# Sums of squares for keys and queries: squares of transposed blocks on ScalarE in place of products with a column of ones

## The chip, the cores and the metric

The kernel runs on one core of one Trainium2 chip. The metric is the device time of one execution in microseconds, here the median of three runs. TensorE does the matrix products (PE in the profile, its weight loads PEld), VectorE is DVE, ScalarE is ACT, GpSimd is POOL, and SP issues the DMAs. All engines run in order; the kernel fixes the order on each of them when it is built.

## What is computed

One decoder layer on x of 1024 tokens by 1024 channels, fp32: a gated DeltaNet branch with 8 heads and a sparse attention branch with 8 heads, merged by gates, an output product, and an MLP of width 4096. The change lies in the DeltaNet branch, in the L2 norm of its queries and keys over the 128 channels of a head:

```python
def l2_normalize(x):
    xf = x.astype(jnp.float32)
    return xf * lax.rsqrt(jnp.sum(xf * xf, axis=-1, keepdims=True) + EPS)
...
    qkv = jax.nn.silu(causal_short_conv(g_qkv, conv_w))
    gq, gk, gv = jnp.split(qkv, [GDN_QK_DIM, 2 * GDN_QK_DIM], axis=-1)
    gq = l2_normalize(gq.reshape(B, S, GDN_HEADS, GDN_HEAD_K)) * (GDN_HEAD_K ** -0.5)
    gk = l2_normalize(gk.reshape(B, S, GDN_HEADS, GDN_HEAD_K))
...
    o_gdn = gated_delta_rule_chunked(gq, gk, gv, g, beta)
```

## The kernel before, in words

The input projection is made in units of 128 or 256 columns, each a chain of products in PSUM tiles called `dd`. For the DeltaNet branch there are 48 units (per head: key `k`, query `q`, value `v`, and the gates `z`, `a`, `b`). Every fp32 operand is split into a high and a low part, so one K-tile of 128 takes three products of 512 columns, and a half unit takes 24 (`gdense`, line 711).

A key, query or value unit goes through `conv` (line 760): ScalarE copies the two halves out of PSUM into `cu`, ScalarE and VectorE make the causal convolution of four taps, ScalarE the Tanh and VectorE the product that is SiLU. The result (`kt`, `qt` or `t` in the profile) has channels on partitions and the 1024 tokens along the free axis. For keys and queries `conv` then takes the sums of squares over the channels, that is over partitions (lines 800 to 812): ScalarE squares the whole tile into `cu` (128x1024), TensorE multiplies each of the eight blocks of 128 tokens with a column of ones (`one`, 128x1) into a tile of the PSUM ring `tt`, and VectorE reads the eight columns of sums, adds epsilon (4 * EPS) and gives the tile back. Then `conv` is done, and `keys` (line 823), `queries` (line 982) or `values` (line 1002) of that head starts.

`keys` fetches a row of decays by DMA (`es`), has ScalarE make the decay matrix, takes the reciprocal root of the sums (`rsq_w`), the products of keys with keys (`tt<-kt`), and hands 32x32 blocks through DRAM to a solve on POOL (`sx`, `stmp`, `um`). `join` puts the blocks of the inverse together (`jj`). `decayed` transposes the keys (`tt<-ident,kt`) for the state's update. `queries` makes the products of queries with keys (`tt<-qt,kt`). `scan` (line 1024) is the recurrence over 8 chunks of a head: `cc` and `oo` on TensorE, `sr` and `sst` on VectorE, `svn`, `sqs` and a square with an accumulator (`gj`) on ScalarE. `output` (line 1078) uses the queries' sums once more, transposes and writes the head out.

The ring `tt` (class `Ring`, two PSUM tiles) is shared by all of these. A chain waits for a free tile (`yield tt.ready`), takes it (`tt.get`) and frees it behind the last reader.

The order of all engines is made by a planner (`Weave`, line 2011). Each step above is a Python generator; the planner keeps a time of its own, books a duration for each instruction by a fixed formula, and takes the ready chain with the smallest priority number. `gdense` has the last priority, 9: its `dd` products fill the time in which no other chain has work for TensorE. What an instruction does on the chip in longer time than the formula makes the plan late there, as the engines follow the planned order and not the planned times. The formulas that matter here:

```python
                if op == "matmul" and not fast and "tile_position" not in kw:
                    return wv.issue(name, ins, (n * 1.67 + 5) / 1e3, 0.25)
...
                return wv.issue(name, ins, (n * (0.417 if fast else 0.835) + (13.4 if wv.shared else 2.5)) / 1e3, 0.25)
...
                return wv.issue(name, ins, 0.13 + n / 1200 + (0.1 if "accum_out" in kw else 0), 0.15)
```

The first is an fp32 product of n columns on TensorE (for n = 1 it books 0.007 us), the second an F32R product or a transpose, the third a ScalarE activation of n elements per partition.

Of the kernel before, what the change touches and what calls it, by code (L numbers as in the profile page):

```python
# [9 lines left out]
F32 = mybir.dt.float32  # L10
F32R = mybir.dt.float32r
BF16 = mybir.dt.bfloat16
F16 = mybir.dt.float16
I32 = mybir.dt.int32
AF = mybir.ActivationFunctionType
OP = mybir.AluOpType
# [4 lines left out]
P = 128  # L21
S = 1024
D = 1024
NB = S // P
# [4 lines left out]
EPS = 1e-6  # L29
# [21 lines left out]
def body(tc, a, out, dbg=None):  # L51
    nc = tc.nc
    ctx = ExitStack()
    V, A, G, PE, SY = nc.vector, nc.scalar, nc.gpsimd, nc.tensor, nc.sync
# [23 lines left out]


    padl, padl_es = pool("padl", side="left")  # L80
    G.memset(padl.tile([P, 24], F32, name="padl"), 0.0)
    cst, cst_es = pool("cst", side="left")
    dr, dr_es = pool("dr", space=DRAM)
    htp, ht_es = pool("htp", side="left")
# [14 lines left out]
    V_, A_, G_, PE_, SY_ = (wv.engine(e, n) for e, n in ((V, "V"), (A, "A"), (G, "G"), (PE, "PE"), (SY, "SY")))  # L99

    def rsq_w(pl, dst, src, n, tag):
        t = pl.tile([P, n], F32, name=tag + "t")
        V_.tensor_scalar(dst.bitcast(I32), src.bitcast(I32), -0.5, float(0x5F3759DF), op0=OP.mult, op1=OP.add)
        for _ in range(3):
            yield
            V_.scalar_tensor_tensor(t, dst, -0.5, src, op0=OP.mult, op1=OP.mult)
            yield
            V_.tensor_tensor(t, t, dst, op=OP.mult)
            yield
            V_.scalar_tensor_tensor(dst, t, 1.5, dst, op0=OP.add, op1=OP.mult)  # L110
# [10 lines left out]
    ident = cst.tile([P, P], F32, name="ident")  # L121
    vecs = cst.tile([P, NV], F32, name="vecs")
    g025 = cst.tile([P, 1], F32, name="g025")
    one = cst.tile([P, 1], F32, name="one")
    dtb = cst.tile([P, H], F32, name="dtb")
    alg = cst.tile([P, H], F32, name="alg")
    nss, nms, nr = (cst.tile([P, NB], F32, name=n) for n in ("nss", "nms", "nr"))
# [31 lines left out]
    def loads():  # L159
        SY_.dma_start(ident, a["c_ident"])  # L160
        after(("ident",))
        for half in range(2):
            if half == 0:
                ts = [ix.tile([P, NB, 256], F32, name="pj", bufs=2).rearrange("p a b -> p (a b)") for _ in range(2)]
                xs.extend(t[:, o:o + D] for t in ts for o in (0, D))
            else:
                xs.extend([slot(1, [P, D], F32), slot(5, [P, D], F32)]
                          + [ix.tile([P, D], F32, name="irl", bufs=2) for _ in range(2)])
            for tb in range(4 * half, 4 * half + 4):
                SY_.dma_start(xs[tb], x[tb * P:(tb + 1) * P, :])  # L170
                after(("x", tb))
            if half == 0:
                SY_.dma_start(vrow[0:96], a["conv_w"][0].rearrange("j (t p) -> (j t) p", p=P))
                SY_.dma_start(vrow[96:104], a["norm_mix_g"][0].rearrange("(t p) -> t p", p=P))
                SY_.dma_start(vrow[104:112], a["norm_mlp_g"][0].rearrange("(t p) -> t p", p=P))
                SY_.dma_start(vrow[112:113], a["gdn_norm_g"])
                after(("vrow",))
                load(0)
                after(("raw", 0))
        load(1)  # L180
        after(("raw", 1))
        SY_.dma_start(ropeI, a["c_ropei"])
        SY_.dma_start(dtb, a["dt_bias"].to_broadcast([P, H]))
        SY_.dma_start(alg, a["a_log"].to_broadcast([P, H]))
        SY_.dma_start(triu, a["c_triu"])
        G_.memset(ones, 1.0)
        G_.memset(one, 1.0)
        SY_.dma_start(ropeA, a["c_ropea"])
        SY_.dma_start(qng, a["q_norm_g"].to_broadcast([P, P]))
        SY_.dma_start(kng, a["k_norm_g"].to_broadcast([P, P]))  # L190
        yield


    def after(key):
        wv.add(0, later(wv.busy["SY"] + SY_LATENCY, key))
# [471 lines left out]
    blk = lambda t, b: t[:, b * P:(b + 1) * P]  # L667
# [92 lines left out]
    def conv(u):  # L760
        h, c = gunits[u]
        ct = ctile[c] + h
        yield ("gp",)
        if len(convs) > 1:
            yield ("conv", convs[-2])
        convs.append(u)
        cu = gq.tile([P, 3 + S], F32, name="cu", bufs=2)
        G_.memset(cu[:, 0:3], 0.0)
        for half in range(2):
            yield ("half", (u, half))  # L770
            wv.add(-1, cdrain(cu, u, half))
            yield ("drained", u, half)
        cw = [vecs[:, j * 24 + ct:j * 24 + ct + 1] for j in range(4)]
        if c == "k" and h > 2:
            yield ("out", h - 3)
        if c == "k" and h > 1:
            yield ("keys", h - 2)
        if c == "q" and h > 1:
            yield ("scan", h - 2)
        if c == "q" and h > 2:  # L780
            yield ("out", h - 3)
        if c == "v" and h:
            yield ("values", h - 1)
        yield
        o = (gq if c == "v" else gp).tile([P, S], F32, name={"k": "kt", "q": "qt", "v": "t4"}[c],
                                          bufs={"k": 3, "q": 2, "v": 1}[c])
        A_.activation(o, cu[:, 0:S], AF.Copy, scale=cw[0])
        for j in range(1, 4):
            yield
            yield "V"  # L790
            V_.scalar_tensor_tensor(o, cu[:, j:j + S], cw[j], o, op0=OP.mult, op1=OP.add)
        yield
        yield "A"
        A_.activation(cu[:, 0:S], o, AF.Tanh, scale=0.5)
        yield
        yield "V"
        V_.scalar_tensor_tensor(o, cu[:, 0:S], 1.0, o, op0=OP.add, op1=OP.mult)
        yield
        st[h][c + "t"] = o
        if c != "v":  # L800
            yield "A"
            A_.activation(cu[:, 0:S], o, AF.Square)
            yield
            yield tt.ready
            ps, slot_ = tt.get()
            for b in range(NB):
                PE_.matmul(ps[:, 0, b:b + 1], blk(cu, b), one, start=True, stop=True)
            yield
            st[h][c + "ss"] = gp.tile([P, NB], F32, name=c + "ss", bufs=3)
            V_.tensor_scalar(st[h][c + "ss"], ps[:, 0, 0:NB], 4 * EPS, None, op0=OP.add)  # L810
            tt.free(slot_)
            yield
        wv.done("conv", u)
        wv.add(2, {"k": keys, "q": queries, "v": values}[c](h))

# [7 lines left out]
    def keys(h):  # L823
# [9 lines left out]
        SY_.dma_start(es.rearrange("p b c -> p (b c)"), GC[h:h + 1, :].to_broadcast([P, S]))  # L833
        dma = ("es", h)
        after(dma)
        yield dma
        for b in range(NB):
            A_.activation(es[:, b, :], es[:, b, :], AF.Abs, bias=ngc[:, b, h:h + 1])
# [2 lines left out]
            if b % 4 == 3:  # L841
                A_.activation(es[:, b - 3:b + 1, :], es[:, b - 3:b + 1, :], AF.Exp, scale=-1.0)
        rk = gp.tile([P, NB], F32, name="rk", bufs=2)
        yield from rsq_w(gp, rk, st[h]["kss"], NB, "rk")
        ck = gp.tile([P, NB], F32, name="ck", bufs=2)
        av = gp.tile([P, NB], F32, name="av", bufs=3)
        nb_ = gp.tile([P, NB], F32, name="nb", bufs=3)
# [55 lines left out]
            SY_.dma_start(um[32 * q:32 * q + 32, :, 32 * q:32 * q + 32], zu[q])  # L903
        yield
        wv.add(1, join(h))


    def decayed(h):
# [73 lines left out]
    def queries(h):  # L982
        qt = st[h]["qt"]
        yield ("keys", h)
        if h > 1:
            yield ("out", h - 2)
        kt, aq = st[h]["kt"], st[h]["aq"]
        for half in range(2):
            hs = slice(half * 4, half * 4 + 4)
            yield tt.ready  # L990
            ps, slot_ = tt.get()
            for i in range(4):
                b = half * 4 + i
                PE_.matmul(ps[:, i, :], blk(kt, b), blk(qt, b), start=True, stop=True)
            yield
            V_.tensor_tensor(aq[:, hs, :], ps, aq[:, hs, :], op=OP.mult)
            tt.free(slot_)
            yield
        wv.done("queries", h)
# [78 lines left out]
    def output(h):  # L1078
        yield ("gate", (h, "a"))
        oss, qss, oo, og = (st[h][k] for k in ("oss", "qss", "vv", "kt"))  # L1080
        fo = gp.tile([P, NB], F32, name="fo", bufs=2)
        fe = gp.tile([P, NB], F32, name="fe", bufs=2)
        V_.tensor_scalar(fe, qss, 128 * EPS, None, op0=OP.mult)
        yield
        V_.scalar_tensor_tensor(fe, oss, 1.0 / P, fe, op0=OP.mult, op1=OP.add)
        yield
        yield from rsq_w(gp, fo, fe, NB, "fo")
        yield
        V_.tensor_tensor(oo, oo, fo[:, :, None].to_broadcast([P, NB, P]), op=OP.mult)
        yield  # L1090
        for half in range(2):
            yield tt.ready
            ps, slot_ = tt.get()
            for i in range(4):
                PE_.transpose(ps[:, i, :], oo[:, half * 4 + i, :], ident)
            yield
            hs = slice(half * HALF, (half + 1) * HALF)
            V_.scalar_tensor_tensor(og[:, hs], ps.rearrange("p a b -> p (a b)"), g025, zzs[h][:, hs],
                                    op0=OP.mult, op1=OP.mult)
            tt.free(slot_)  # L1100
            yield
        SY_.dma_start(M1[h // 4][h % 4], og)
        yield
        wv.done("out", h)
# [1088 lines left out]
```

## Time and profile before

| | |
|---|---|
| median of 3 runs | 1859.11 us (1858.0 to 1859.21) |
| profiled execution, its own time | 1857.71 us |
| its span | 1856.0 us |
| TensorE busy | 1827.3 us (98%) |
| VectorE busy | 1263.4 us (68%) |
| ScalarE busy | 1005.1 us (54%) |
| POOL busy | 548.8 us (30%) |

Read it so: the busy share is an average over the span. Matmuls are pipelined, and the profile models their ends, so two records of TensorE can overlap, and the distance from one start to the next is what a product really takes. The DeltaNet heads run from about 270 to 965 us, the attention and the MLP behind them. Nearly all instructions are issued through one helper and so carry one line number; they are told apart by the names of their tiles, as output<-moving operand, stationary operand for TensorE.

### The profile page before, as it was taken

How to read it: one execution, taken by the hardware profiler on the slowest of the kernel's cores; microseconds unless marked ns; L12 is line 12 of the kernel's file. 1: busy time of each engine (PE TensorE's matmuls, PEld its weight loads, DVE VectorE, ACT ScalarE, POOL GpSimd, SP SyncE). 2: the span in 40 equal slices, each digit the busy share in tenths (PEclk: the TensorE clock that was granted, in tenths of full speed). 3: DMA queues.
4: the chain of work that ended last, by engine and by line, in shares of the span. 5: the costliest groups of instructions: out<-in, count | busy, mean ns of one | idle time of the engine just before them, and what ended most of it. 6: DMA issues, size and time to landing. Idle time of an engine off the chain costs nothing.

```text
span 1856.0 us, 28461 instructions
## 1 busy us (share of the span) xinstructions
PE 1827.3 (98%) x10406; PEld 1560.9 (84%) x10406; DVE 1263.4 (68%) x2615; ACT 1005.1 (54%) x2022; POOL 548.8 (30%) x752
## 2 busy tenths in 40 slices
PE   8899999999999999999999999999999999999999
PEld 7889998888888888888888888877888888888887
DVE  4557757757677777865348767677866667957655
ACT  6556646646566555354237666666666665333330
POOL 0214640542524516356003311231232322222210
PEclk8999999999999999999999999999999999999999
DMA  4102232233122222321336412222644459453423
GB/s 160 47 25 68 69 103 57 63 90 78 50 69 58 58 57 69 87 63 49 86 122 212 147 60 66 80 97 75 208 143 155 157 180 328 150 188 102 125 79 137
DMA packets 190510, 195.65 MB, mean 105 GB/s; under 512 B 36593, under 2 KB 140322, under 8 KB 190370
## 3 DMA queue, kind: packets, MB, share of 16 engines
q1 hardware_dynamic: 190370, 193.83, 33.3%
q8 instruction: 82, 1.34, 0.3%
q14 instruction: 58, 0.48, 0.1%
HBM read 139.62 MB, written 54.17 MB: 104 GB/s over the span
## 4 chain that ended last, share of the span: by engine, by line
PE 93%; DVE 3%; ACT 1%; issue 1%; POOL 0%; DMA 0%; SPq 0%; DVEq 0%; POOLq 0%; ACTq 0%
PE dd L2122 54%; PE o L2122 14%; PE s L2122 7%; PE pt L2122 6%; PE tt L2122 4%; PE cc L2122 2%; PE jj L2122 2%; PE sq L2122 2%; PE oo L2122 1%; DVE w L2122 1%; DVE rqs L2122 1%; PE tp L2122 0%; DVE sc L2122 0%; DMA pj<-in_x_dram 0%; POOL hl L2122 0%
## 5 line engine op out<-in xcount | busy, mean ns | idle before, releaser
L2122 PE MATMUL dd<-hh,w 128*128 128x512 f32 x1568 | 521.3, 403 | 0.9 <-ACT hh L2122 0.9
L2122 PEld LDWEIGHTS dd<-hh,w 128*128 128x128 f32 x1568 | 288.8, 189 | 52.2 <-ACT hh L2122 1.3
L2122 PE MATMUL dd<-hl,w 128*128 128x512 f32 x784 | 316.2, 403 | 0.6 <-DVE hl L2122 0.6
L2122 PE MATMUL dd<-w,hh 128*128 128x256 f32 x960 | 182.8, 287 | 0.0
L2122 ACT ACTIVATE m<-m 128x512 f32<-128x512 f32 (+1 forms) x240 | 140.0, 625 | 76.6 <-PE dd L2122 32.4
L2122 PE MATMUL dd<-hh,m 128*128 128x512 f32 x520 | 172.0, 395 | 1.0 <-DVE w L2122 0.8
L2122 PEld LDWEIGHTS dd<-hl,w 128*128 128x128 f32 x784 | 148.1, 189 | 26.5 <-DVE hl L2122 1.5
L2122 DVE TENSOR_TENSOR m<-m,m 128x512 fp32r<-128x512 f32 (+2 forms) x177 | 134.9, 790 | 36.1 <-ACT m L2122 33.0
L2122 PEld LDWEIGHTS dd<-w,hh 128*128 128x128 f32 x960 | 154.8, 194 | 1.5
L2122 PE MATMUL dd<-w,hl 128*128 128x256 f32 x480 | 137.4, 286 | 0.0
L2122 POOL TENSOR_TENSOR sx<-sx,stmp 128x60 f32<-128x60 f32 (+24 forms) x248 | 114.4, 461 | 19.4
L2122 PEld LDWEIGHTS dd<-hh,m 128*128 128x128 f32 x520 | 96.7, 188 | 20.5 <-DVE w L2122 2.4
L2122 POOL TENSOR_TENSOR stmp<-sx,um 128x60 f32<-128x60 f32 (+24 forms) x186 | 82.9, 446 | 76.0 <-DMA um<-ZA 62.6
L2122 POOL TENSOR_TENSOR m<-m,m 128x512 f32<-128x512 f32 x48 | 67.6, 1417 | 126.3 <-ACT m L2122 62.1
L2122 DVE TENSOR_SCALAR_CACHE_REDUCE tkeq<-sc,cand 128x384 f16<-128x384 f32 (+3 forms) x128 | 103.3, 807 | 1.4
L2122 PE MATMUL dd<-hl,m 128*128 128x512 f32 x260 | 102.3, 393 | 0.9 <-POOL hl L2122 0.9
L2122 DVE TENSOR_TENSOR w<-w,w 128x1024 fp32r<-128x1024 f32 (+1 forms) x56 | 65.4, 1172 | 47.1 <-ACT w L2122 47.1
L2122 PEld LDWEIGHTS dd<-w,hl 128*128 128x128 f32 x480 | 93.2, 194 | 0.1
L2122 ACT ACTIVATE ha<-m 128x1024 fp32r<-128x1024 f32 x43 | 43.8, 1054 | 80.0 <-PE s L2122 35.3
L2122 ACT ACTIVATE hh<-m 128x1024 fp32r<-128x1024 f32 x40 | 40.7, 1055 | 75.1 <-PE o L2122 37.6
L2122 ACT ACTIVATE w<-w 128x1024 fp32r<-128x1024 f32 x48 | 50.8, 1058 | 55.1 <-PE dd L2122 52.2
L2122 PE MATMUL o<-hh,m 128*128 128x512 f32 x248 | 80.3, 391 | 0.0
(468 smaller groups left out, 4456.2 us busy)
## 6 DMA issues: line engine op xcount, KB each, us to landing
HD<-m SPq DMA_DIRECT2D x106, 256.0 KB, 2.3
m<-HD SPq DMA_DIRECT2D x53, 512.0 KB, 3.9
w<-in_w_in_dram SPq DMA_DIRECT2D x48, 512.0 KB, 4.0
m<-in_w_mlp_up_dram SPq DMA_DIRECT2D x33, 512.0 KB, 5.1
wraw<-in_w_in_dram SPq DMA_DIRECT2D x8, 1024.0 KB, 5.3
m<-in_w_mlp_down_dram SPq DMA_DIRECT2D x16, 512.0 KB, 4.4
w<-in_x_dram SPq DMA_DIRECT2D x10, 512.0 KB, 4.9
hh<-in_w_mlp_down_dram SPq DMA_DIRECT2D x10, 512.0 KB, 4.7
```

The costliest lines, as they stand in the source:

```text
L2122: ins = f(*args, **kw)
```

## The change

The sums are taken at another place and by other engines. `conv` ends with the SiLU. A new helper `squares` transposes the eight blocks of a key or query tile, four to a tile of the ring `tt`, so that tokens are on partitions; ScalarE squares each block of 128x128 from PSUM and adds up along the free axis with its accumulator (`accum_out`). `keys` calls it behind the issue of the decay row, `queries` at its start. Epsilon is added by an extra operation for the keys (`ke`) and inside an operation that was there for the queries (`fe`). The column of ones goes; the pad at the start of SBUF grows from 24 to 32 columns.

```diff
-    G.memset(padl.tile([P, 24], F32, name="padl"), 0.0)
+    G.memset(padl.tile([P, 32], F32, name="padl"), 0.0)
...
         st[h][c + "t"] = o
-        if c != "v":
-            yield "A"
-            A_.activation(cu[:, 0:S], o, AF.Square)
-            yield
-            yield tt.ready
-            ps, slot_ = tt.get()
-            for b in range(NB):
-                PE_.matmul(ps[:, 0, b:b + 1], blk(cu, b), one, start=True, stop=True)
-            yield
-            st[h][c + "ss"] = gp.tile([P, NB], F32, name=c + "ss", bufs=3)
-            V_.tensor_scalar(st[h][c + "ss"], ps[:, 0, 0:NB], 4 * EPS, None, op0=OP.add)
-            tt.free(slot_)
-            yield
         wv.done("conv", u)
...
         after(dma)
+        kss = gp.tile([P, NB], F32, name="kss", bufs=2)
+        yield from squares(kt, kss)
         yield dma
...
-        yield from rsq_w(gp, rk, st[h]["kss"], NB, "rk")
+        ke = gp.tile([P, NB], F32, name="ke", bufs=2)
+        V_.tensor_scalar(ke, kss, 4 * EPS, None, op0=OP.add)
+        yield
+        yield from rsq_w(gp, rk, ke, NB, "rk")
...
+    def squares(t, ss):
+        for half in range(2):
+            yield tt.ready
+            ps, slot_ = tt.get()
+            for i in range(4):
+                PE_.transpose(ps[:, i, :], blk(t, half * 4 + i), ident)
+            yield
+            for i in range(4):
+                b = half * 4 + i
+                junk = gp.tile([P, P], BF16, name="gj")
+                A_.activation(junk, ps[:, i, :], AF.Square, accum_out=ss[:, b:b + 1])
+                if i % 2:
+                    yield
+            tt.free(slot_)
...
         kt, aq = st[h]["kt"], st[h]["aq"]
+        qss = st[h]["qss"] = gp.tile([P, NB], F32, name="qss", bufs=3)
+        yield from squares(qt, qss)
...
-        V_.tensor_scalar(fe, qss, 128 * EPS, None, op0=OP.mult)
+        V_.tensor_scalar(fe, qss, 4 * EPS, 128 * EPS, op0=OP.add, op1=OP.mult)
```

Since the planner books other durations and other chains, the order moves on every engine between the first key and the end of the last head's recurrence. On TensorE the first 1803 rows and the last 3588 rows of the order (rows of equal instructions merged) are the same before and after. The first place is TensorE at the first key's sums, among the `dd` products of the next unit; before:

```order
L2122 MATMUL dd<-hl_113,w_3182 128x512
L2122 MATMUL dd<-hh_112,w_3183 128x512
L2122 MATMUL tt<-one,cu 128x1 x8
L2122 MATMUL dd<-hh_98,w_3182 128x512
L2122 MATMUL dd<-hl_99,w_3182 128x512
L2122 MATMUL dd<-hh_98,w_3183 128x512
L2122 MATMUL dd<-hh_100,w_3182 128x512
L2122 MATMUL dd<-hl_101,w_3182 128x512
L2122 MATMUL dd<-hh_100,w_3183 128x512
L2122 MATMUL dd<-hh_102,w_3182 128x512
L2122 MATMUL tt<-ident,kt 128x128 x4
```

With the change, the second half of the same key (the first half stands 15 `dd` products earlier, in one row of eight with the first half of `decayed`):

```order
L2130 MATMUL dd<-hh_111,w_3180 128x512
L2130 MATMUL dd<-hl_112,w_3180 128x512
L2130 MATMUL tt<-ident,kt 128x128 x4
L2130 MATMUL dd<-hh_111,w_3181 128x512
L2130 MATMUL dd<-hh_97,w_3180 128x512
L2130 MATMUL dd<-hl_98,w_3180 128x512
L2130 MATMUL dd<-hh_97,w_3181 128x512
L2130 MATMUL dd<-hh_99,w_3180 128x512
L2130 MATMUL tt<-ident,kt 128x128 x4
```

The group of eight products with `one` is gone, and there are twice as many groups of four transposes of `kt`, one for the squares and one for `decayed`. Over the program 16 groups of 8 products go and 32 groups of 4 transposes come, nearly all of them standing alone among `dd` products.

The second place is ScalarE at the first steps of the first head's recurrence (`svn` is the copy on which TensorE's next two products wait, `es` the next head's decay matrix, `th` a gate's Tanh, `tkcm` a count of the attention's search); before:

```order
L2122 ACTIVATE svn<-cc 128x128
L2122 ACTIVATE gj,oss<-vv 128x128
L2122 ACTIVATE es<-es,ngc 128x128 x2
L2122 ACTIVATE sqs<-oo,eg 128x128
L2122 ACTIVATE es<-es,ngc 128x128 x2
L2122 ACTIVATE svn<-cc 128x128
L2122 ACTIVATE es<-es 128x512
```

With the change:

```order
L2130 ACTIVATE svn<-cc 128x128
L2130 ACTIVATE gj,kss<-tt 128x128 x4
L2130 ACTIVATE gj,oss<-vv 128x128
L2130 ACTIVATE sqs<-oo,eg 128x128
L2130 ACTIVATE gj,kss<-tt 128x128 x2
L2130 ACTIVATE svn<-cc 128x128
L2130 ACTIVATE gj,kss<-tt 128x128 x2
L2130 ACTIVATE es<-es,ngc 128x128 x2
L2130 ACTIVATE th<-dd 128x512
```

The eight squares of the next head's keys now stand between the recurrence steps of this head, where two halves of the decay matrix stood. Of the 64 `svn` rows of the program 22 have such squares between them and the `svn` before, and 11 have them in the row directly ahead.

## Rows read from the trace of the kernel before

**Rows 1.** The page: busy time, the chain that ended last, granted clock in 40 slices.
```profile
PE 1827.3 (98%) x10406; PEld 1560.9 (84%) x10406; DVE 1263.4 (68%) x2615; ACT 1005.1 (54%) x2022; POOL 548.8 (30%) x752
...
PEclk8999999999999999999999999999999999999999
...
PE 93%; DVE 3%; ACT 1%; issue 1%; POOL 0%; DMA 0%; SPq 0%; DVEq 0%; POOLq 0%; ACTq 0%
```

**Rows 2.** Table by stretch: length, then PE, PEld, DVE, ACT, POOL busy, clock, DMA.
```profile
285.00:900.00 615.00, 614.58 (x3918) 523.13 (x3918) 436.18 (x1127) 333.17 (x749) 249.50 (x546) 1.00 0.25 65
860.00:965.00 105.00, 105.00 (x640) 88.65 (x640) 45.44 (x100) 38.57 (x95) 17.39 (x35) 1.00 0.27 76
965.00:1856.00 891.00, 882.00 (x4157) 731.61 (x4155) 626.21 (x1064) 481.57 (x846) 209.81 (x130) 1.00 0.43 142
```

**Rows 3.** TensorE's waits, 285 to 960 us: us in total, times, longest.
```profile
PE tt L2122 <- DVE es L2122: 0.4, 1, 0.4
```

**Rows 4.** Tile `tt`, TensorE: ns min/median/max, first and last start in us, forms.
```profile
L2122 PE MATMUL tt<-one,cu x256: 164/250/250, 294.1 to 860.4; 128*128 128x1 f32 x128
...
L2122 PE MATMUL tt<-ident,kt x64: 270/272/328, 297.5 to 826.3; 128*128 128x128 f32 x64
```

**Rows 5.** TensorE in order of time, 293 to 299 us: start, us, what, count.
```profile
293.90 0.39 PE L2122 MATMUL dd<-hh,w 128*128 128x512 f32 x1
294.13 1.84 PE L2122 MATMUL tt<-one,cu 128*128 128x1 f32 x16
295.83 0.48 PE L2122 MATMUL dd<-hh,w 128*128 128x512 f32 x1
296.15 0.39 PE L2122 MATMUL dd<-hl,w 128*128 128x512 f32 x1
296.37 0.62 PE L2122 MATMUL dd<-hh,w 128*128 128x512 f32 x2
...
297.51 0.60 PE L2122 MATMUL tt<-ident,kt 128*128 128x128 f32 x4
297.87 0.48 PE L2122 MATMUL dd<-hl,w 128*128 128x512 f32 x1
298.18 0.63 PE L2122 MATMUL dd<-hh,w 128*128 128x512 f32 x2
298.65 0.40 PE L2122 MATMUL dd<-hl,w 128*128 128x512 f32 x1
```

**Rows 6.** Groups of instructions, TensorE, whole span: busy us, mean ns, idle before.
```profile
L2122 PE MATMUL tt<-one,cu 128*128 128x1 f32 x256 | 29.5, 245 | 0.0
...
L2122 PE MATMUL tt<-ident,kt 128*128 128x128 f32 x64 | 9.6, 273 | 0.4 <-DVE es L2122 0.4
```

**Rows 7.** Groups of instructions, ScalarE, 285 to 960 us.
```profile
L2122 ACT ACTIVATE cu<-kt 128x1024 f32<-128x1024 f32 x16 | 16.9, 1056 | 7.2 <-DVE kt L2122 4.1 <-DVE cand L2122 3.1
L2122 ACT ACTIVATE cu<-qt 128x1024 f32<-128x1024 f32 x16 | 16.9, 1056 | 1.9 <-DVE qt L2122 1.9
```

**Rows 8.** ScalarE in order of time: squares with accumulator of another stage, one after another.
```profile
203.04 0.31 ACT L2122 ACTIVATE hj<-iq 128x128 bf16<-128x128 f32 x1
203.25 0.18 ACT L2122 ACTIVATION_READ_ACCUMULATOR hj<-iq 128x1 f32 x1
203.47 0.31 ACT L2122 ACTIVATE hj<-iq 128x128 bf16<-128x128 f32 x1
```

**Rows 9.** In order of time: an `svn` on ScalarE, then the product that waits for it.
```profile
725.18 0.28 ACT L2122 ACTIVATE svn<-cc 128x128 f32<-128x128 f32 x1
...
725.84 0.38 PE L2122 MATMUL cc<-svn,kd 128*128 128x128 f32 x2
```

**Rows 10.** The first solve's result: SP's issues, VectorE's pick-up, landing of tile `um`.
```profile
392.77 1.86 SPq L2122 DMA_DIRECT2D um<-ZU  x4
...
399.21 1.31 DVE L2122 STREAM_TRANSPOSE t<-um 32x256 f32<-32x256 f32 x3
...
DMA to landing us min/median/max: 1.7/2.0/5.0
```

More of the change, by code (lines that the diff above doesn't have):

```diff
@@ L123, in body @@
     g025 = cst.tile([P, 1], F32, name="g025")
-    one = cst.tile([P, 1], F32, name="one")
     dtb = cst.tile([P, H], F32, name="dtb")
@@ L186, in loads @@
         G_.memset(ones, 1.0)
-        G_.memset(one, 1.0)
         SY_.dma_start(ropeA, a["c_ropea"])
```

## The prediction

> **What bounds the kernel now.** I read the page first, then a table by stage, then the waits of TensorE alone. The page's busy line gives TensorE 1827.3 of 1856.0 us, the chain that ended last is 93% PE, and the granted clock stays at 9 tenths or more after the first slice [rows 1]. A busy TensorE need not be a full one, so the second look is for waiting: between 285 and 900 us, the stretch that holds everything the change touches, TensorE is busy 614.58 of 615.00 us at a granted clock of 1.00, that is at the 2.4 GHz level, while ScalarE is busy 333.17 us [rows 2]. The list of TensorE's waits between 285 and 960 us has a single entry, 0.4 us [rows 3]. So in this stage TensorE never stands still: the projection products `dd` (F32R, 512 columns) fill every hole between the small steps of the eight heads. After 965 us it is busy 882.00 of 891.00 us [rows 2], so what is saved here is not eaten later, provided the later order is the same, which it is: the last 3588 rows of TensorE's order agree. A microsecond of TensorE work taken from this stage is a microsecond off the end, unless TensorE starts to wait.
>
> **What the change removes on TensorE.** 16 groups (8 heads, key and query) of 8 products with the column of ones. The trace has them as 256 matrix passes, two per product [rows 4]. They have one moving column each, so by columns they would be free, but each pass still loads 128x128 weights. The time a group really takes is read from starts, because ends of matmuls are modelled: first pass at 294.13, next `dd` product at 295.83, so 1.70 us; the `dd` product right behind it takes 0.32 us (295.83 to 296.15) where its neighbours take 0.22 [rows 5]. That is 1.80 us a group, and 16 x 1.80 = **28.8 us** removed. The sum of their busy time, 29.5 us, says the same [rows 6].
>
> **What it adds on TensorE.** 32 groups of 4 transposes of a 128x128 block. The same operation is in the trace: `tt<-ident,kt`, of which a group of four starts at 297.51 and the next `dd` at 297.87, 0.36 us, with 0.31 us for that `dd` against 0.23 in the pair behind it (298.18 to 298.65): 0.44 us a group [rows 5]. A transpose is one pass where an fp32 product is two: 64 records for 64 transposes [rows 4]. 32 x 0.44 = **14.1 us** added. Two prices bound this. The group row has 9.6 us for 16 such groups [rows 6], 0.60 us each, 19.2 us for 32; it counts the modelled tail under which the next product already runs, so it is an upper end. 0.36 us each, 11.5 us, is the lower. Net on TensorE: 28.8 - 14.1 = **-14.7 us**, between -10.3 (29.5 - 19.2) and -18.0 (29.5 - 11.5). I take the middle since it is measured start to start with the neighbour's delay in it.
>
> **ScalarE.** Removed are 16 squares of 128x1024, 1.06 us each (the two groups `cu<-kt` and `cu<-qt` hold 16 each, half of them Tanh): 16.9 us [rows 7]. Added are 128 squares of 128x128 with an accumulator, each followed by the read of that accumulator. In a row of such squares one starts 0.43 us after the other (203.04, 203.47) [rows 8]: 55.0 us. ScalarE's load in the stage rises by 38 us from 333.17 of 615 us, 54% to 60%. It has the room on average; this costs the end nothing by itself. Cover gone, it would cost what TensorE waits for it. That is the uncertain term. The planner that laid out the order books 0.13 + 128/1200 + 0.10 = 0.337 us for such a square, and the row says 0.43, so four of them come about 0.4 us late against the plan. In the new ScalarE order 22 of the 64 recurrence steps (`svn`) have such squares between them and the step before; 11 have them directly in front. Behind `svn` TensorE waits in order with `cc<-svn,kd`, and everything behind that waits too. The tightest such pair in the trace ends at 725.18 + 0.28 = 725.46 on ScalarE and starts at 725.84 on TensorE: 0.38 us of room [rows 9]. 0.4 us of lateness just uses that up. I book **+1 us** of new waits, between 0 and 22 x 0.3 = 6.6 us (eight squares late by 0.8 us, less 0.4 to 0.5 of room, at every one of the 22).
>
> **The rest.** VectorE loses 16 tiny reads of the sums and gets 8 additions of epsilon; it was not waited for, nothing. The query's epsilon rides in an operation that was there: nothing. `conv` reports done one square, one group of products and one read earlier, so a head's work may start earlier; TensorE has no hole for it to fill, so nothing. The squares of the keys stand in `keys` behind the issue of the decay row's DMA, so they run under its flight. SP and POOL issue what they issued, in a slightly other order between heads. POOL drops one memset of the ones column at the start, and the pad that replaces it is as long as what went; nothing.
>
> **Sum.** -14.7 + 1.0 = -13.7 us on the profiled execution of 1857.7 us gives 1844.0 us. The median of the runs, 1859.1, lies 1.4 above that execution, so I forecast **1845.4 us**.
>
> **Rivals.**
> *Half of it is given back* (ScalarE late at the recurrence). For it: the 0.4 us of lateness against 0.38 us of room. And a cover goes: the planner books 8 x 0.007 us for a group of ones that takes 1.80, so at 16 places the other engines had some 1.7 us that no plan gave them; transposes it books at 0.12 us each, about what they take. Against: of the 22 places 11 have another ScalarE step between, and in the 105 us behind the last group of ones (it starts at 860.4 [rows 4]) TensorE was busy 105.00 us [rows 2], so the plan holds without that cover too. 1859.1 - 14.7 + 6.6 = 1851.0.
>
> *Slower: the two PSUM tiles of the ring `tt` become the bound.* A sum used to be taken off by one short VectorE read; now a tile is held for four squares, and keys, products, values and outputs of all heads share the two tiles. TensorE is in order, so a pass that finds no tile stops the filler as well. If square and accumulator read do not overlap at all they take 0.31 + 0.19 = 0.50 us [rows 8], 4 x (0.50 - 0.337) = 0.65 us beyond the plan, and met at each of the 32 groups 20.8 us: 1859.1 - 14.7 + 20.8 = 1865.2. It decides from 14.7 / 32 = 0.46 us of wait per group. Against: the starts in the row show 0.43, not 0.50, and nearly all the new groups stand apart in the order with several `dd` products between.
>
> *Slower: a transpose costs its full record.* A transpose's record lasts 272 ns [rows 4]; if the chip ran them one behind the other, 128 x 0.272 = 34.8 us would come for 29.5 us: +5.3, 1864.4. Against: four of them merge into 0.60 us and the next product starts 0.36 us after the first [rows 5]. The Trainium skill, "TensorE: Matmul & The Clock Gate", section "Part 4: PE-mode transpose", puts a 128x128 bf16 transpose at about 275 ns in one kernel's context; by that rule 128 of them would be an estimated 35 us, and the change a loss. The trace agrees with the length of one and not with such a spacing.
>
> *No change: another chain has the end.* If the heads' order were tied to the solve on POOL, TensorE would only wait longer for it. The net saving is 14.7 / 8 = 1.8 us a head. The solve's last DMAs of the first head are issued by 392.77 + 1.86 = 394.63, land about 2.0 us later (the median there), and VectorE picks them up at 399.21: 2.6 us of room [rows 10], enough; the other heads have more. 1859.1.
>
> **Chances.** The forecast's case (1841.5 to 1848.5) 0.73; half given back 0.11; no change 0.07; the ring 0.06; the full transpose 0.03. The range takes the forecast's bounds and the half case with some 2 us beyond it: 1841.5 to 1853, which leaves out less than 2 in 10. 0.2% is 3.7 us, about what a measurement of this kernel can tell from no change; so faster is 0.73 + 0.11 = 0.84, same 0.07, slower 0.09.
>
> **What would show it.** In the new profile: no `one` in any TensorE row; 128 `tt<-ident,kt` and 64 `tt<-ident,qt`, whose four starts still take 0.36 us; the first product of the attention stage about 13 us earlier; TensorE's waits between 285 and 950 us still in a list of some 1 us; 128 squares `gj<-tt` on ScalarE, its busy time up by about 40 us. I am wrong if that list names ScalarE's `svn` or `gj` with several us (half given back), if `tt` heads it (the ring), or if TensorE's busy time in the stage falls by less than 10 us.

## The result, and the profile after

The changed kernel takes 1843.78 us, the median of five runs (1841.87 to 1845.76), where the kernel before takes 1859.11 us in five runs beside it (1857.84 to 1860.01): a ratio of 0.9919, interval 0.9907 to 0.993, 15.3 us less. The forecast was 1845.4 us. The profiled execution of the changed kernel took 1841.87 us, its span 1840.1 us.

From the page of the changed kernel, the lines that answer to [rows 1]:

```profile
PE 1812.0 (98%) x10278; PEld 1545.6 (84%) x10278; DVE 1264.9 (69%) x2607; ACT 1028.7 (56%) x2262; POOL 540.9 (29%) x751
...
PEclk9999999999999999999999999999999999999999
...
PE 93%; DVE 3%; ACT 1%; issue 1%; POOL 1%; DMA 0%; SPq 0%; DVEq 0%; POOLq 0%; ACTq 0%
```

TensorE lost 128 records net, as it should: 256 passes of `one` went, 128 transposes came. Its busy time fell by 15.3 us, the time by as much, and the share of the chain did not move: TensorE bounds the kernel as before.

The table by stretch of the changed kernel (columns as in [rows 2]):

```profile
285.00:900.00 615.00, 614.58 (x3935) 519.47 (x3933) 440.98 (x1125) 361.28 (x997) 241.80 (x546) 1.00 0.25 68
950.00:1840.10 890.10, 881.07 (x4152) 730.83 (x4151) 625.58 (x1063) 481.01 (x845) 209.65 (x130) 1.00 0.43 143
```

TensorE again has no hole between 285 and 900 us. The list of its waits from 285 to 945 us in the changed kernel has the one entry of [rows 3] and nothing new:

```profile
PE tt L2130 <- DVE es L2130: 0.4, 1, 0.4
```

How much shorter did the stage get? Two marks that stand at the same place in both orders tell: the first copy `cu<-dd`, and the first product of the attention, `s<-ident,ql`. Rows of these two tiles (ns min/median/max, then first and last start in us), the kernel before:

```profile
L2122 ACT ACTIVATE cu<-dd x48: 577/599/609, 272.6 to 864.1; 128x512 f32<-128x512 f32 x48
...
L2122 PE MATMUL s<-ident,ql x64: 270/272/275, 970.0 to 1175.9; 128*128 128x128 f32 x64
```

And of the changed kernel:

```profile
L2130 ACT ACTIVATE cu<-dd x48: 575/598/626, 271.1 to 842.4; 128x512 f32<-128x512 f32 x48
...
L2130 PE MATMUL s<-ident,ql x64: 270/272/273, 953.9 to 1159.9; 128*128 128x128 f32 x64
```

From mark to mark it was 970.0 - 272.6 = 697.4 us and is 953.9 - 271.1 = 682.8: **14.6 us less**. Behind the second mark it was 1856.0 - 970.0 = 886.0 us and is 886.2: nothing given back. The other 1.5 us lie ahead of the first mark, where the order is the same; that mark lies between 271.0 and 274.6 us over all the runs below, so I count none of it for the change. I call the two pieces "stage" and "rest" from here on.

Do the marks enclose the same work? The `dd` products between them, before and then changed (length, TensorE busy with `dd` and their count, clock, DMA share, GB/s):

```profile
272.60:970.00 697.40, 576.04 (x2210) 1.00 0.26 71
271.10:953.90 682.80, 577.28 (x2210) 1.00 0.26 72
```

The same 2210 products, at a granted clock of 1.00, the 2.4 GHz level, in both. Where an experiment lets the planner lay out the order anew, this count moves: each `dd` product that changes sides takes some 0.23 us [rows 5] from one piece to the other, and the stage has to be read with that in mind.

### The profile page after: what moved, and what is told of

Its sections match the earlier page's. It is cut to its first block, busy times and chain, and to the rows that moved or that the text cites. A ratio compares the mean times of both kernels' runs of the same rounds, so it can differ in the third digit from the quotient of the medians.

```text
span 1840.1 us, 28462 instructions
## 1 busy us (share of the span) xinstructions
PE 1812.0 (98%) x10278; PEld 1545.6 (84%) x10278; DVE 1264.9 (69%) x2607; ACT 1028.7 (56%) x2262; POOL 540.9 (29%) x751
## 4 chain that ended last, share of the span: by engine, by line
PE 93%; DVE 3%; ACT 1%; issue 1%; POOL 1%; DMA 0%; SPq 0%; DVEq 0%; POOLq 0%; ACTq 0%
PE dd L2130 54%; PE o L2130 15%; PE s L2130 7%; PE pt L2130 6%; PE tt L2130 4%; PE cc L2130 2%; PE jj L2130 2%; PE sq L2130 2%; PE oo L2130 1%; DVE w L2130 1%; DVE rqs L2130 1%; PE tp L2130 1%; DVE sc L2130 0%; DMA pj<-in_x_dram 0%; DVE hl L2130 0%
## 5 line engine op out<-in xcount | busy, mean ns | idle before, releaser
L2130 DVE TENSOR_TENSOR m<-m,m 128x512 fp32r<-128x512 f32 (+2 forms) x177 | 135.3, 792 | 35.8 <-ACT m L2130 32.7
L2130 POOL TENSOR_TENSOR sx<-sx,stmp 128x60 f32<-128x60 f32 (+24 forms) x248 | 106.1, 428 | 19.4
L2130 POOL TENSOR_TENSOR stmp<-sx,um 128x60 f32<-128x60 f32 (+24 forms) x186 | 73.9, 397 | 84.9 <-DMA um<-ZA 71.2
L2130 ACT ACTIVATE tkcm<-sc,cand 128x896 f16<-128x896 f32 x64 | 69.9, 1091 | 17.5 <-DVE cand L2130 15.1
```

What stands on the lines that cost most here:

```text
L2130: ins = f(*args, **kw)
```

## The experiments

All runs in one table. Each ratio is to runs of the kernel before on the same chip, whose medians lie between 1858.68 and 1859.11 us. A difference to the changed kernel is taken to after_again; where the chip was another one, some 0.3 us of it can be the chip's. Stage and rest are read from the profiled execution, as above.

| run | median us | ratio (95% interval) | stage | rest |
|---|---|---|---|---|
| kernel before | 1859.11 | | 697.4 | 886.0 |
| changed kernel | 1843.78 | 0.9919 (0.9907 to 0.993) | 682.8 | 886.2 |
| after_again | 1843.45 | 0.9916 (0.9903 to 0.993) | 682.8 | 886.1 |
| transposes_twice | 1872.5 | 1.0072 (1.0059 to 1.0084) | 694.1 | 903.4 |
| squares_twice | 1864.64 | 1.0031 (1.0019 to 1.0042) | 685.7 | 904.6 |
| q_left_out | 1841.77 | 0.9906 (0.9893 to 0.992) | 680.2 | 886.8 |
| ones_booked | 1866.65 | 1.0046 (1.0033 to 1.0059) | 709.0 | 886.4 |
| ones_twice | 1930.25 | 1.039 (1.0376 to 1.0404) | 771.6 | 888.8 |
| keys_shared | 1875.95 | 1.0092 (1.0076 to 1.0107) | 711.0 | 889.1 |
| transposes_kept | 1858.21 | 0.9997 (0.9988 to 1.0006) | 696.8 | 886.2 |
| q_kept | 1837.4 | 0.9885 (0.9871 to 0.9898) | 676.2 | 886.5 |
| squares_kept | 1872.96 | 1.0072 (1.0059 to 1.0085) | 710.6 | 886.1 |
| shared_two | 1842.63 | 0.9913 (0.9898 to 0.9928) | 681.1 | 886.1 |

**The changed kernel once more (after_again)**, without an edit, as the base of the next three.

> The changed kernel once more, as the mark for the three runs beside it. Both theories: 15 us less than the kernel before (it was 15.3), within 1.5 us.

1843.45 us, and the same 682.8 and 886.1 us. The gain repeats.

**Each term doubled, the plan left to itself.** First the transposes for the squares:

```diff
-            for i in range(4):
+            for i in (0, 1, 2, 3, 0, 1, 2, 3):
                 PE_.transpose(ps[:, i, :], blk(t, half * 4 + i), ident)
```

> The changed kernel with each of the 32 groups of four transposes made twice into the same PSUM tile; ScalarE's work is the same. Theory 1 (the time is TensorE's work, start to start): a transpose takes 0.09 us inside a group, so four more in a group that stands alone take 0.36 us; 32 x 0.36 = 11.5 us over the changed kernel, 3.5 to 4 us under the kernel before. Rival (a transpose costs its record of 272 ns): 128 x 0.272 = 34.8 us over the changed kernel.

It took 29 us more than the changed kernel, more than twice what was expected. The stage gives +11.3 us, the rest +17.3, though the transposes were added to the stage alone. The planner had booked them, and so laid out everything behind them in another order. The trace says what that did: 10 `dd` products moved behind the second mark (2200 against 2210 in the stage), some 2.3 us; TensorE stands idle for 17.5 us of the rest where it was 9.0; and the granted clock falls to 0.50 three times there, 3.4 us each, which by (1 - clock) x time is up to 5.1 us. At the same work the stage is 11.3 + 2.3 = 13.6 us longer. As a whole this run prices the order, not the transposes.

Then the squares:

```diff
+                for _ in range(2):
-                A_.activation(junk, ps[:, i, :], AF.Square, accum_out=ss[:, b:b + 1])
+                    A_.activation(junk, ps[:, i, :], AF.Square, accum_out=ss[:, b:b + 1])
```

> The changed kernel with each of the 128 squares on ScalarE made twice; TensorE's work is the same. It adds 128 x 0.43 = 55 us of ScalarE work in a stage of some 600 us, and holds each tile of the ring about 1.7 us longer. Theory 1 (ScalarE's work is hidden, the ring is not the bound): within 2 us of the changed kernel. Rival (ScalarE gives part of the gain back already, or the ring of two tiles does): what is given back at least doubles, 5 us or more over the changed kernel, and TensorE's list of waits between 285 and 950 us names svn or tt with several us.

+21.2 us, of which 2.9 in the stage and 18.5 in the rest. Here too the order moved: 15 `dd` products, some 3.5 us, went from the stage to the rest (2195 against 2210), so at the same work the stage is 6.4 us longer. In it TensorE stands idle for 3.0 us against 0.4, for ScalarE's `t`, `am` and `um` and not for the squares, and the clock is at 0.50 from 467 to 477 us, up to 5.1 us. So what 128 more squares cost when planned for can't be told from this run.

And the queries' sums left out:

```diff
-        yield from squares(qt, qss)
+        V_.memset(qss, 1.0)
```

> The changed kernel without the queries' sums of squares: their 16 groups of transposes and 64 squares are left out, and the sums are set to one. Theory 1 (TensorE's work alone): 16 x 0.44 = 7.0 us less than the changed kernel. Rival (ScalarE or the ring gives back part): more than 9 us less, since that part goes too.

Only -1.7 us, with 2.6 in the stage. The order moved the other way: 16 `dd` products more, some 3.7 us, had been done ahead of the second mark (2226), so at the same work the stage is 6.3 us shorter, near the expected 7.0; in the rest TensorE stands idle for 12.2 us where it was 9.0. Three misses of one kind: in this kernel an edit that the planner sees is two edits.

**The old way, booked at its true time (ones_booked)**, on the kernel before. The prediction held that the groups of ones gave other engines time that no plan had counted; this takes the cover away by telling the planner:

```diff
-                    return wv.issue(name, ins, (n * 1.67 + 5) / 1e3, 0.25)
+                    return wv.issue(name, ins, 0.213 if n == 1 else (n * 1.67 + 5) / 1e3, 0.25)
```

> The kernel before, in which only the planner's formula is changed: a product with the column of ones is booked at 0.213 us, what it takes, instead of 0.007. The order moves, the work stays. Theory 1 (the gain is TensorE's work): no change against the kernel before, within 2 us. Rival (the gain came from the better planned order, as the new operations are booked at what they take): part of the 15 us, 4 us or more below the kernel before.

7.8 us slower, which neither theory had. Its table by stretch, in steps of 5 us (columns as in [rows 2]):

```profile
455.00:460.00 5.00, 5.00 (x23) 4.13 (x22) 4.45 (x14) 4.67 (x8) 0.00 (x0) 1.00 0.34 73
460.00:465.00 5.00, 5.00 (x59) 4.40 (x58) 3.95 (x7) 3.60 (x7) 0.00 (x0) 0.92 0.55 160
465.00:470.00 5.00, 5.00 (x56) 4.15 (x56) 4.99 (x12) 0.78 (x3) 4.15 (x10) 0.50 0.28 109
470.00:475.00 5.00, 5.00 (x24) 3.79 (x23) 0.52 (x2) 1.14 (x3) 3.98 (x14) 0.50 0.01 3
475.00:480.00 5.00, 5.00 (x28) 3.68 (x28) 2.34 (x3) 1.94 (x3) 4.22 (x11) 0.72 0.00 0
480.00:485.00 5.00, 5.00 (x38) 4.66 (x37) 1.30 (x6) 1.71 (x8) 3.98 (x14) 1.00 0.01 2
```

TensorE is busy all the time, yet its granted clock goes from 1.00 to 0.50, the 1.2 GHz level. Ahead of the fall the new order had put a group of ones right behind small products. TensorE of this kernel in order of time:

```profile
461.70 1.09 PE L2122 MATMUL jj<-um,am 32*32 32x32 f32 x32
462.72 2.25 PE L2122 MATMUL tt<-one,cu 128*128 128x1 f32 x16
464.83 1.09 PE L2122 MATMUL tt<-ident,vv 128*128 128x128 f32 x4
```

A clock of 0.92 over 460 to 465 us is 0.8 us at 0.50, so it falls at about 464.2, within the group, which takes 464.83 - 462.72 = 2.11 us where it took 1.70 [rows 5]. The loss, (1 - clock) x time, is 5 x (0.08 + 0.50 + 0.50 + 0.28) = 6.8 us here, and a second fall at 860 to 870 us adds 1.7: 8.5 of the 1869.1 - 1857.71 = 11.4 us by which this profiled execution lies over that of before. The stage, 11.6 us longer than before, holds 16 `dd` products more (2226 against 2210), some 3.7 us; with the clock's 8.5 that is 12.2, so nothing is left for the uncounted cover in it. The rest, with those products gone, is as long as before because TensorE stands idle for 12.1 us there instead of 9.0. So booking the old way rightly gave no gain of its own, in this one order.

**The old way twice (ones_twice)**, on the kernel before:

```diff
+                for _ in range(2):
-                PE_.matmul(ps[:, 0, b:b + 1], blk(cu, b), one, start=True, stop=True)
+                    PE_.matmul(ps[:, 0, b:b + 1], blk(cu, b), one, start=True, stop=True)
```

> The kernel before with each of the 128 products with the column of ones made twice. Theory 1: a product takes 1.70 / 8 = 0.213 us inside a group, so 128 x 0.213 = 27.2 us over the kernel before. Rival (a product with one column costs by its columns, and what went away was something else, as the wait or the square of 128x1024): under 5 us.

+71.4 us. The first doubled group takes 297.25 - 292.60 = 4.65 us, the fourth 366.08 - 362.60 = 3.48. TensorE in order of time:

```profile
292.60 4.79 PE L2123 MATMUL tt<-one,cu 128*128 128x1 f32 x32
297.25 0.77 PE L2123 MATMUL dd<-hh,w 128*128 128x512 f32 x1
...
362.60 3.63 PE L2123 MATMUL tt<-one,cu 128*128 128x1 f32 x32
366.08 0.47 PE L2123 MATMUL dd<-hl,w 128*128 128x512 f32 x1
366.40 0.95 PE L2123 MATMUL dd<-hh,w 128*128 128x512 f32 x2
```

The clock in the same two stretches (length, PE busy, clock, DMA share, GB/s):

```profile
293.00:294.00 1.00, 1.00 (x11) 1.00 1.12 393
294.00:295.00 1.00, 1.00 (x10) 0.91 0.47 180
295.00:296.00 1.00, 1.00 (x7) 0.50 0.03 12
...
300.00:301.00 1.00, 1.00 (x5) 0.50 0.00 0
301.00:302.00 1.00, 1.00 (x6) 0.68 0.00 0
302.00:303.00 1.00, 1.00 (x6) 1.00 0.00 0
...
362.00:366.00 4.00, 4.00 (x36) 1.00 0.26 78
```

The mean granted clock of the whole span is 0.975, against 0.994 before. The loss by it is 0.025 x 1931.4 - 0.006 x 1856.0 = 37 us, and with the 27.2 expected that is 64 of the 75 us by which this profiled execution (1933.08 us) lies over that of before. A price can still be read, from the groups that end ahead of a fall: seven of the 16 do, six of them as long as the fourth within 0.01 us, one 3.59. So 16 more passes behind 16 others, at the 2.4 GHz level, take 3.48 - 1.70 = 1.78 us, and 16 times that is 28.5, where the prediction had 28.8 for the groups. The stage agrees to some 2 us: 52 `dd` products more ahead of its end (2262 against 2210, some 12.0 us), 35.8 us by the clock and 28.5 for the passes are 76.3 of 74.2 us.

**One transposition for two uses (keys_shared)**, on the changed kernel. `decayed` transposes the same keys once more; here ScalarE takes the square and the scaled copy from one tile, which saves 16 groups. The keys then have to wait for one of the two buffers of the decayed keys, held by the recurrence two heads before:

```diff
-        wv.add(3, decayed(h))
...
-        yield from squares(kt, kss)
+        if h > 1:
+            yield ("scan", h - 2)
+        kd = gp.tile([P, NB, P], F32, name="kd", bufs=2)
+        yield from squares(kt, kss, kd, h)
+        st[h]["kd"] = kd
+        wv.done("decayed", h)
...
                 A_.activation(junk, ps[:, i, :], AF.Square, accum_out=ss[:, b:b + 1])
+                if kd is not None:
+                    A_.activation(kd[:, b, :], ps[:, i, :], AF.Copy, scale=egd[:, b, h:h + 1])
```

> A candidate to beat both: the changed kernel, in which the keys are transposed once instead of twice. The tile of the ring that the squares read is read by the copies that make the decayed keys as well, so 16 groups of four transposes go. The decayed keys have two buffers, so a head's keys now start only when the recurrence of two heads before is done. Theory 1: 16 x 0.44 = 7.0 us less than the changed kernel, 22 us less than the kernel before, if TensorE still finds filler. Rival (the later start of the keys makes the chain through the solve the bound): the gain is eaten, the same as the changed kernel or slower, and TensorE's waits name jj or cc.

32 us slower than the changed kernel: the rival held, and worse. From its list of TensorE's waits, 285 to 985 us:

```profile
PE dd L2116 <- ACT cu L2116: 10.8, 2, 7.9
```

The filler itself stops: a finished unit waits for ScalarE to copy it out. In the wait of 7.9 us (612.4 to 620.3 us) ScalarE is not idle; squares, copies of keys and steps of a decay matrix, among others, stand ahead of that copy in its order. That the later start of the keys put them there is argued from the edit, not tried. Waits of 10.8 us are a third of the loss; the mean clock is 0.985, which by the reckoning above is 0.015 x 1874.7 - 0.006 x 1841.2 = 17 us more. The work that was saved is in there all the same: 71 `dd` products, some 16 us, have moved ahead of the second mark (2281), so the lengths of stage and rest say little by themselves.

**The same questions with the order held.** In the next three the planner books nothing for what is added (by a flag), or books what is left out without issuing it; every other row of TensorE's order is that of the changed kernel.

```diff
+        if self.free:
+            dur, lat, port = 0.0, 0.0, False
```

*transposes_kept* issues a second set of four transposes into the same tile between `wv.free = True` and `wv.free = False`:

```diff
             for i in range(4):
                 PE_.transpose(ps[:, i, :], blk(t, half * 4 + i), ident)
+            wv.free = True
+            for i in range(4):
+                PE_.transpose(ps[:, i, :], blk(t, half * 4 + i), ident)
+            wv.free = False
```

> The changed kernel with the 32 groups of four transposes made twice, as before, but the added ones are booked at nothing, so every engine keeps the changed kernel's order to the end. Theory 1 (TensorE's work, start to start, alone): 32 x 0.36 = 11.5 us over the changed kernel, all of it before the attention starts, and the tail as long as the changed kernel's 886 us. Rival (a doubled group has a price beyond its work, by waits or by the clock, and the 29 us seen with a moved order came from that): 20 us or more.

14.8 us over after_again, 14.0 in the stage, nothing in the rest, and TensorE's waits unchanged. That is 14.0 / 32 = 0.44 us for four more transposes behind four others. My expectation was lower because I had counted 0.09 us for each added transpose. Its TensorE in order of time has eight in a row:

```profile
332.00 1.03 PE L2137 MATMUL tt<-ident,qt 128*128 128x128 f32 x8
332.79 0.70 PE L2137 MATMUL dd<-hh,w 128*128 128x512 f32 x2
```

332.79 - 332.00 = 0.79 us for eight where four took 0.36: 0.109 us for each more. That this is as much as the prediction has for a group by itself, 0.36 and 0.08 of its neighbour's delay, is by chance: the added four delay no neighbour a second time. The price of whole groups is read from the next run.

*q_kept* leaves the queries' transposes and squares out and books their times, so the order stays:

```diff
-        yield from squares(qt, qss)
+        yield from booked(qss)
```

> The changed kernel without the transposes and squares of the queries (sums set to one), but with their time still booked, so the order of everything else is kept. Theory 1: 16 x 0.44 = 7.0 us less than the changed kernel. Rival (the 1.7 us seen with a moved order is what a group is worth): under 3 us less. Second rival (ScalarE's squares cost TensorE time as well): over 9 us less.

-6.1 us against after_again, -6.6 in the stage. With the order free the same edit gave -1.7. That is 6.6 / 16 = 0.41 us for a group with its neighbour's delay, where the prediction has 0.44. The 64 squares that went from ScalarE as well show no price of their own: 16 groups of transposes at 0.44 are 7.0 already.

*squares_kept* squares each block twice, the second time unbooked:

```diff
                 A_.activation(junk, ps[:, i, :], AF.Square, accum_out=ss[:, b:b + 1])
+                wv.free = True
+                A_.activation(junk, ps[:, i, :], AF.Square, accum_out=ss[:, b:b + 1])
+                wv.free = False
```

> The changed kernel with each square on ScalarE made twice and the second booked at nothing, so the order is kept and ScalarE comes late against it by 0.43 us a square. Theory 1 in its full form (ScalarE's squares are hidden since the plan makes room for them, some 0.4 to 0.6 us at a recurrence step): 96 squares stand ahead of 21 steps behind the first, 41 us of lateness less 10 us of room: 10 to 30 us over the changed kernel, and TensorE's waits name cc, oo or tt. Rival (ScalarE is idle 40% of the stage, so its work is free wherever it stands): within 2 us.

+29.5 us, 27.8 of them in the stage. The head of its list of TensorE's waits, 285 to 975 us (us in total, times, longest):

```profile
PE tt L2136 <- ACT gj L2136: 10.2, 11, 1.4
PE oo L2136 <- ACT svn L2136: 3.8, 3, 1.8
PE cc L2136 <- ACT svn L2136: 3.4, 6, 1.1
```

These are the two waits that the rivals named, the ring `tt` and the recurrence behind `svn`; they come when ScalarE has 128 squares that the plan does not know. The whole list is 18.8 us, and the clock, at 0.50 for 3.4 us from 831, is 1.7; the remaining 7 of the 27.8 us I can't place.

**Sharing where nothing waits (shared_two).** The edit of keys_shared for the first two heads alone, whose buffers are free from the start:

```diff
-        wv.add(3, decayed(h))
+        if h > 1:
+            wv.add(3, decayed(h))
...
-        yield from squares(kt, kss)
+        if h > 1:
+            yield from squares(kt, kss)
+        else:
+            kd = gp.tile([P, NB, P], F32, name="kd", bufs=2)
+            yield from squares(kt, kss, kd, h)
+            st[h]["kd"] = kd
+            wv.done("decayed", h)
```

> A candidate to beat both: the changed kernel, in which the first two heads' keys, for which a buffer is free anyway, are transposed once for squares and decayed keys; the other heads stay. Four groups of four transposes go. Theory 1: 4 x 0.44 = 1.8 us less than the changed kernel. Rival (the moved order costs or gains more than that): anything from 3 us less to 5 us more.

The stage is 1.7 us shorter, four groups at 0.44. The median is 0.8 us under after_again, and the two intervals cover each other, so a gain over the changed kernel is not shown.

## Why the prediction was right

**TensorE without a hole, so its work counts one for one.** Held. The wait list of the stage is unchanged and the rest kept its length; its order in the last 3588 rows was the same. The experiments in which that order moved show how much hung on this: +17.3 and +18.5 us in the rest, by idle time of TensorE, falls of its clock and a few `dd` products.

**The net of the two prices, -14.7 us.** Measured -14.6 in the stage. The transposes are there as foretold. Tile `tt` of the changed kernel (columns as in [rows 4]):

```profile
L2130 PE MATMUL tt<-ident,kt x128: 270/272/328, 289.1 to 806.7; 128*128 128x128 f32 x128
L2130 PE MATMUL tt<-ident,qt x64: 270/272/275, 328.3 to 843.2; 128*128 128x128 f32 x64
...
L2130 ACT ACTIVATE gj<-tt x128: 255/277/312, 290.9 to 846.3; 128x128 bf16<-128x128 f32 x128
```

And a group of four on its TensorE in order of time, to be held against [rows 5]:

```profile
293.38 0.60 PE L2130 MATMUL tt<-ident,kt 128*128 128x128 f32 x4
293.73 0.71 PE L2130 MATMUL dd<-hh,w 128*128 128x512 f32 x2
```

Four starts take 293.73 - 293.38 = 0.35 us. q_kept puts the price of a whole group at 0.41 by the length of the stage, against 0.44. For the removed group, 1.80 by [rows 5], ones_twice has 1.78 at a clock of 1.00; those are 16 passes behind 16 others, and no run took a group away by itself. With 1.78, the net is 32 x 0.41 - 16 x 1.78 = -15.4 us, or -14.4 with 0.44, and the stage gave -14.6: the two terms hold, and not only their difference.

**ScalarE: mis-sized, though it did not matter.** The step said +38 us of load and four squares late by 0.4 us, and booked +1 us of waits for it. Busy time rose by 1028.7 - 1005.1 = 23.6 us, and no wait came, so the +1 us is the term that was mis-sized; it measured nothing. The pace of 0.43 us in [rows 8] is that of squares in a row. In the changed kernel they often stand in pairs, with other work behind. Its ScalarE in order of time:

```profile
406.49 0.28 ACT L2130 ACTIVATE gj<-tt 128x128 bf16<-128x128 f32 x1
406.67 0.19 ACT L2130 ACTIVATION_READ_ACCUMULATOR gj<-tt 128x1 f32 x1
406.89 0.28 ACT L2130 ACTIVATE gj<-tt 128x128 bf16<-128x128 f32 x1
407.07 0.19 ACT L2130 ACTIVATION_READ_ACCUMULATOR gj<-tt 128x1 f32 x1
407.16 0.27 ACT L2130 ACTIVATE svn<-cc 128x128 f32<-128x128 f32 x1
```

The second square follows the first after 0.40 us, but `svn` follows the second after 0.27: an activation without an accumulator runs beside the read. A pair takes 0.67 us, 2 x 0.335, which is what the planner books (0.337). So by these rows the plan was not late, and 128 x 0.335 - 16.9 = +26 us is near the measured load. Of the 1.6 us by which the forecast lies over the median, this is 1; the rest is no more than the start-up differs from run to run.

The room behind `svn` was read too wide. TensorE's weight load for the product (PEld) starts ahead of it, and in squares_kept it waits for `svn` as the product does. Of the kernel before, beside [rows 9]; of the changed kernel, its tightest pair; of squares_kept, with the wait in brackets:

```profile
725.61 0.42 PEld L2122 LDWEIGHTS cc<-svn,kd 128*128 128x128 f32 x2
...
568.01 0.27 ACT L2130 ACTIVATE svn<-cc 128x128 f32<-128x128 f32 x1
568.42 0.42 PEld L2130 LDWEIGHTS cc<-svn,kd 128*128 128x128 f32 x2
...
510.50 0.26 ACT L2136 ACTIVATE svn<-cc 128x128 f32<-128x128 f32 x1
510.81 0.30 PEld L2136 LDWEIGHTS cc<-svn,kd 128*128 128x128 f32 x2 [1.43 <-ACT svn L2136]
```

To the load it was 725.61 - 725.46 = 0.15 us, not 0.38. In the changed kernel it is still 568.42 - 568.28 = 0.14, where a load that waits starts 0.05 behind `svn`. So 0.4 us of lateness would have cost more than the step had; it did not come.

**The rivals.** *Half given back*: did not happen; no wait behind `svn`. The mechanism exists, as squares_kept shows, but needs lateness that this plan does not have. Nor did a lost cover show: ones_booked, which books the groups of ones at what they take, has no gain by it in the stage. *The ring `tt`*: did not happen; no wait on `gj`, though squares_kept shows that one can come. *The full transpose*: the record lasts 272 ns, the spacing is 0.109 us. The Trainium skill, "TensorE: Matmul & The Clock Gate", section "Part 4: PE-mode transpose", has about 275 ns for one of bf16 data; the trace, with fp32 data, agrees with that as the length of one. As a price it was refuted: by an estimate from that page the 128 added transposes of transposes_kept would have cost 35 us, and they cost 14.0 in the stage. *Another chain*: did not happen; the stage shrank by all that TensorE saved.

## What to carry to other kernels

Where one engine has no hole in a stage, price an edit by distances between starts on that engine, the neighbour's delay included, and the end follows to a few tenths of a microsecond; records of single instructions would have had the wrong sign here. Work moved to an engine with room is free only as long as whatever orders the instructions knows its true time: the change's own 128 squares, planned for, made TensorE wait no longer than before, and 128 more that the plan did not know made the stage 27.8 us longer. And where a planner sets the order, an experiment must hold the order, or count the work on both sides of its mark and the falls of the clock; else it measures several things at once.

## What was not expected of the hardware

The granted clock can fall to 0.50 while TensorE is busy 100% by its records. It did so 15 times in the stage of ones_twice, each time within a group of 32 passes with one moving column or a few products behind one, and in ones_booked within a group of 16 such passes that stood directly behind 32 products of 32x32, and once just behind a group of 16 and 16 products `jj`. (In transposes_twice, squares_twice, keys_shared and squares_kept it also fell where TensorE had stood idle.) Behind single groups of 16 among `dd` products, as in the kernel before, it stayed at 1.00 [rows 2], and so it did with eight transposes in a row in transposes_kept (mean clock 0.994). The Trainium skill, "TensorE: Matmul & The Clock Gate", section "Part 1: The HAM clock gate", says that the clock follows how busy the engine has been; in these rows it fell while the profile has the engine busy without a break. That the small products are to blame is read from what stands ahead of the falls; it was not tried by itself. By (1 - clock) x time it cost 37 of 75 us in ones_twice and 8.5 of 11.4 in ones_booked.
